# Seven half-size products from the seventh unit on in the second and third FFN of a two-layer hybrid model

## The chip, the cores and the metric

The kernel runs on one core of a Trainium2 chip. The metric is the device time of one execution in microseconds (us). The engines are PE (TensorE, matrix products; PEld is its weight load), DVE (VectorE), ACT (ScalarE), POOL (GpSimd) and SP (SyncE, which here only issues transfers). A transfer between the chip's memory (HBM) and the on-chip buffers is a DMA. Each engine works through its own queue in order; when an instruction waits, those behind it wait too.

## The reference

Two layers act on 256 latent tokens (LAT) and 256 context tokens (CTX), 1024 wide. Each layer is a half FFN, a mixer (attention in the first layer, an mLSTM in the second), and another half FFN; the mLSTM and the last FFN have an output for the latent tokens only. Nine modulation vectors per layer come from two condition vectors.

```python
def half_ffn(h, shift, scale, gate, w_in, w_out, g, b):
    xm = modulate(h, shift, scale)
    a, u = jnp.split(xm @ w_in, 2, axis=-1)
    y = (jax.nn.silu(a) * u) @ w_out
    return post_norm(h, 0.5 * gate * y, g, b)

for i in range(DEPTH):
    mod_lat = jnp.split((jax.nn.silu(c) @ ada_w[i] + ada_b[i])[:, None, :], N_MOD, axis=-1)
    mod_ctx = jnp.split((jax.nn.silu(c_ctx) @ ada_w[i] + ada_b[i])[None, None, :], N_MOD, axis=-1)
    h_lat = half_ffn(h_lat, mod_lat[0], mod_lat[1], mod_lat[2], ffn_w_in[i, 0], ffn_w_out[i, 0], ...)
    h_ctx = half_ffn(h_ctx, mod_ctx[0], ...)
    ...
    # mixer on modulated tokens, post_norm
    ...
    h_lat = half_ffn(h_lat, mod_lat[6], mod_lat[7], mod_lat[8], ffn_w_in[i, 1], ffn_w_out[i, 1], ...)
```

`w_in` is 1024 x 5632 (the halves `a` and `u`), `w_out` 2816 x 1024.

## The kernel before

**Precision.** A product of two float32 values is made of three passes in a reduced format (fp32r). Each operand is split into a high part (`h`, a rounding copy on ACT) and a low part (`l = x - h`, a subtraction on DVE): `split`, lines 221 to 227. `mm3` (line 236) then adds h h, h l and l h on PE. Weights arrive by a DMA on SP in chunks of 128 x 1024 values (512 KB) in `raw` buffers (`RAW`, three of them), and are split into a pair `w` (`WB`, seven of them).

**An FFN** (`ffn`, line 658) works on 22 units of 128 hidden columns, in two halves of 11 (`hf` 0 and 1). A full unit (`unit_in`) takes two weight chunks: 16 blocks of 128 x 128, each in three passes over all 512 tokens, 48 products of 512 columns. `ffn_g` makes silu(a) u and splits it. Behind each half, `unit_out` multiplies the 11 results by `w_out` for eight output blocks `d` of 33 products each. The first four units of the second and third FFN (LEAD) run on the latent tokens first and then on the context tokens, while the norm of the stage before still ends.

**Seven products.** In the second half (units 11 to 21) of the second and third FFN, `fast_in` (line 606) treats a unit as a 2 x 2 by 2 x 2 block product (a against u, lower against upper half of the 1024 inputs, latent against context tokens) with seven half-size products in place of eight. These are 7 x 4 x 3 = 84 products of 256 columns. It needs sums of weight blocks (line 615, four per unit, on DVE), all seven of them split (four splits), and sums of token blocks (`fast_sums`, line 579), which were made beside the output blocks 4 and 5 of the first half. At the end of a unit, lines 649 to 656 put the products together on DVE and ACT.

**Modulation.** Two layers of `ada_w` have 144 chunks of 512 KB. `ada` (line 343) loads one on SP into one of two `ada` buffers and forms a dot product on DVE for each condition vector (line 337). The 72 chunks of the second layer (112 dots) run inside the second and third FFN, as `DOTS` says: 4 or 3 dots per full unit, and some per output block. The silu of the condition vectors (`cb`) was held beside the `ada` buffers; that memory was given up for the token sums of `fast_in` and loaded again after each FFN.

**Order.** The kernel is written as one stream; a scheduler orders each engine's queue when it is built, by the order of the text and by when it expects operands and free buffers. `pin` keeps instructions in the order of the text. The residual (`residual`, line 536: DVE line 543, ACT line 544) runs as two per unit from unit 4 on. A weight pair is free once PE has made its last product with it; the next cast (line 222) waits for that.

**mLSTM** (`mlstm`, line 1146): queries, then keys (`jobs`, the convolution at lines 1179 and 1180), then values (line 1229), then a loop over eight head and direction units (`inner`, `outer`, `gated`; lines 1250 to 1324), then the output product.

Of the kernel before, what the change touches and what calls it, by code (L numbers as in the profile page):

```python
# [42 lines left out]
RAW = 3  # L43
# [92 lines left out]
def part_k(part, k):  # L136
    return k // 4 * 8 + part * 4 + k % 4


class Stream:  # L140


    def __init__(self, b, chunks, sh=0):
        self.b, self.chunks, self.kept = b, chunks, (None, None)
        self.sh = sh if callable(sh) else lambda c: sh

    def __call__(self, i, w=P):
        c, o = divmod(i * P, 1024)
        if self.kept[0] != c:
            self.kept = (c, self.b.chunk(self.chunks[c], self.sh(c)))  # L150
        h, l = self.kept[1]
        return h[:, o : o + w], l[:, o : o + w]
# [17 lines left out]
class Body:  # L170
# [44 lines left out]
    def chunk(self, src, sh=0):  # L215
        r = self.raw(src)
        h, l = self.pair(sh=sh)
        self.split(r, h, l)
        return h, l

# [48 lines left out]
    def setup(self):  # L269
# [13 lines left out]
        self.s1 = {}  # L283

    def silu_c(self):

        pool = ExitStack()
        self.n += 1
        p = pool.enter_context(self.tc.tile_pool(name=f"cp{self.n}", bufs=1, side="right"))
        self.cp = p  # L290
        self.cb = self.t([P, 2, D], pool=p)
        return pool
# [4 lines left out]

    def silu_all(self):
        pool = self.silu_c()
        self.silu_load()  # L300
        self.silu()
        return pool
# [24 lines left out]
    def ada_load(self, layer, dt):  # L327
        if (layer, dt // ND) not in self.mod:
            self.mod[layer, dt // ND] = self.t([P, 2, ND])
        r = self.t([P, 1024], tag="ada", bufs=2, pool=self.cp)  # L330
# [64 lines left out]
    def add_sum(self, g, d):  # L395
# [4 lines left out]
        if d == 0:  # L400
            self.s1[g] = self.t([P, TL], tag="s1", bufs=S1B)
# [21 lines left out]
    def norm(self, g, coef, keep=True, nxt=True, alone=False):  # L423
# [20 lines left out]
        for d in range(ND):  # L444
# [16 lines left out]
            else:  # L461
                a, s2 = sums[eng]
                s2 = s2 or self.t([P, TL], tag="s1", bufs=S1B)
# [30 lines left out]
        if most:  # L494
            dls = self.t([P, TL], tag="dl", bufs=1)
# [10 lines left out]
        if raw:  # L506
            S.copy(rs, rb[:, :w])
            dr = self.t([P, TL], tag="s1", bufs=S1B)
# [37 lines left out]

    def ffn_g(self, j, pa, pu, g, raw=False):
# [3 lines left out]
        if j not in self.gt:  # L551
            self.gt[j] = tuple(self.t([P, self.gw], F32R, tag=k, bufs=self.gn, pool=self.gp) for k in ("gh", "gl"))
        gh, gl = self.gt[j]
# [18 lines left out]
    def fast_operands(self, st):  # L572
# [3 lines left out]
        at = [2 * i * n + (FLIP if i == 2 else 0) for i in range(3)]  # L576
        self.made = [[x[:, a + p * n : a + (p + 1) * n].rearrange("p (k f) -> p k f", f=TL) for p in range(2)] for a in at]

    def fast_sums(self, i):
# [1145 lines left out]
```

## Time and profile before

| | |
|---|---|
| median of 3 runs | 1650.65 us (1648.48 to 1651.94) |
| the profiled execution | 1649.32 us, of it 1647.6 us from the first to the last instruction (the span) |
| granted PE clock, mean | 0.993 |
| products on PE | 10308 |
| read from HBM | 249.81 MB |
| first FFN, attention | to about 385, to about 590 us |
| second FFN, third FFN | to about 930, to about 1275 us |
| mLSTM, last FFN | to about 1460 us, to the end |

The profile is a record of one execution. In a list of groups, a row has the line, the engine, the operation, output and input, the shape and the count, then busy time, mean duration in ns and the idle time before it with what ended it. In a timeline, a row begins with the start and the length in us; an entry in brackets is the idle time of the engine before it and what it waited for. In windows, each engine's busy time in the stretch is followed by the number of its instructions. A duration is not always the distance to the next start: instructions of one engine overlap a little.

### The profile page before, as it was taken

The numbers are of one execution on the slowest core, as the hardware profiler recorded it, in microseconds if no ns is written. First come the engines' busy times: TensorE is split into PE (matmuls) and PEld (weight loads), VectorE is DVE, ScalarE is ACT, GpSimd is POOL, SyncE is SP. The second block draws the span as 40 slices with busy tenths as digits, with TensorE's granted clock in tenths as the row PEclk, the third lists the DMA queues.
The fourth block names the chain that finished last, engine by engine and source line by source line (L and its number), as shares of the span: only waits on it lengthen the run. The fifth ranks groups of instructions, "written<-read, shape, count | busy, mean of one in ns | idle before, by whom it ended". The sixth has DMA issues, their size and how long they took to land. (4 is left out here: it accounts for less than half of the span.)

```text
span 1647.6 us, 26587 instructions
## 1 busy us (share of the span) xinstructions
PE 1617.8 (98%) x10308; PEld 1457.4 (88%) x10308; DVE 1353.8 (82%) x2689; ACT 744.2 (45%) x1269; POOL 61.6 (4%) x76
## 2 busy tenths in 40 slices
PE   9999999999999999999999999899999999999998
PEld 6888888899988998889999998689999989999987
DVE  5899978649888879999977977799965968897687
ACT  5532222314676343425652433225652656656542
POOL 0000000001011200000000100000000100020000
PEclk9999999999999999999999999899999999999999
DMA  9577765622103247733353267733352342437652
GB/s 371 187 237 231 239 215 187 203 76 84 65 1 91 64 143 229 229 128 129 103 182 126 78 193 255 250 120 116 115 155 66 116 120 78 135 109 256 181 172 96
DMA packets 72495, 252.59 MB, mean 153 GB/s; under 512 B 7984, under 2 KB 10800, under 8 KB 72368
## 3 DMA queue, kind: packets, MB, share of 16 engines
q1 hardware_dynamic: 71792, 250.10, 47.8%
q8 instruction: 81, 1.33, 0.3%
q10 hardware_dynamic: 576, 0.79, 0.1%
q14 instruction: 46, 0.38, 0.1%
HBM read 249.81 MB, written 1.05 MB: 152 GB/s over the span
## 5 line engine op out<-in xcount | busy, mean ns | idle before, releaser
L238 PE MATMUL t<-t,t 128*128 128x256 f32 (+2 forms) x8412 | 1325.1, 319 | 14.2 <-ACT t L222 10.7
L238 PEld LDWEIGHTS t<-t,t 128*128 128x128 f32 x8412 | 1193.1, 189 | 133.9 <-ACT t L222 12.7
L222 ACT CAST t<-t 128x1024 fp32r<-128x1024 f32 (+3 forms) x521 | 429.6, 844 | 467.3 <-PE t L238 244.3
L227 DVE TENSOR_TENSOR t<-t,t 128x256 fp32r<-128x256 f32 (+2 forms) x740 | 514.7, 728 | 116.6 <-ACT t L222 112.5
L337 DVE SCALAR_TENSOR_TENSOR t<-t,t 128x1024 bf16<-128x1024 f32 x224 | 263.5, 1220 | 25.2 <-DMA t<-in_ada_w 24.5
L909 PE MATMUL t<-t,t 128*128 128x256 f32 (+1 forms) x256 | 79.5, 311 | 0.0
L911 PE MATMUL t<-t,t 128*128 128x256 f32 (+1 forms) x256 | 78.8, 308 | 0.0
L910 PE MATMUL t<-t,t 128*128 128x256 f32 (+1 forms) x256 | 78.4, 306 | 0.0
L568 ACT ACTIVATE t<-t 128x512 f32<-128x512 f32 (+1 forms) x71 | 34.3, 487 | 95.6 <-PE t L238 95.6
L692 DVE SCALAR_TENSOR_TENSOR t<-t,t,t 128x256 f32<-128x256 f32 x96 | 42.7, 478 | 37.0 <-PE t L238 37.0
L569 DVE TENSOR_TENSOR t<-t,t 128x512 f32<-128x512 f32 (+1 forms) x71 | 38.9, 551 | 32.8 <-PE t L238 26.7
L464 POOL TENSOR_TENSOR t<-t,t 128x256 f32<-128x256 f32 x30 | 23.4, 781 | 1130.9 <-ACT t L454 1129.7
L1424 PE MATMUL t<-t,t 128*128 128x512 f32 (+3 forms) x286 | 60.2, 365 | 2.0 <-ACT t L1501 1.0
L837 PE MATMUL t<-t,t 128*128 128x512 f32 (+1 forms) x300 | 60.7, 364 | 0.0
L1424 PEld LDWEIGHTS t<-t,t 128*128 128x128 f32 (+2 forms) x286 | 43.8, 159 | 18.3 <-issue 2.2
L837 PEld LDWEIGHTS t<-t,t 128*128 128x128 f32 x300 | 51.4, 189 | 9.1 <-DVE t L831 0.3
L454 ACT ACTIVATE t<-t 128x256 f32<-128x256 f32 x72 | 26.2, 411 | 72.3 <-DVE t L447 72.3
L544 ACT ACTIVATE t<-t,t 128x256 f32<-128x256 f32 x64 | 29.4, 503 | 57.4 <-DVE t L543 57.4
L909 PEld LDWEIGHTS t<-t,t 128*128 128x128 f32 x256 | 48.4, 189 | 2.7
L910 PEld LDWEIGHTS t<-t,t 128*128 128x128 f32 x256 | 48.2, 188 | 2.6
L911 PEld LDWEIGHTS t<-t,t 128*128 128x128 f32 x256 | 48.1, 188 | 2.5
L615 DVE TENSOR_TENSOR t<-t,t 128x512 f32<-128x512 f32 x66 | 45.3, 686 | 1.1 <-DMA t<-in_ffn_in 0.3
(200 smaller groups left out, 1065.5 us busy)
## 6 DMA issues: line engine op xcount, KB each, us to landing
t<-in_ffn_in SPq DMA_DIRECT2D x168, 512.0 KB, 4.1
t<-in_ada_w SPq DMA_DIRECT2D x137, 512.0 KB, 4.2
t<-in_ffn_out SPq DMA_DIRECT2D x66, 512.0 KB, 4.4
t<-in_ffn_last SPq DMA_DIRECT2D x22, 512.0 KB, 3.5
t<-in_att_in SPq DMA_DIRECT2D x12, 512.0 KB, 3.5
t<-in_c SPq DMA_DIRECT2D x8, 512.0 KB, 7.8
t<-in_att_out SPq DMA_DIRECT2D x8, 512.0 KB, 3.5
t<-in_ml_qk SPq DMA_DIRECT2D x8, 512.0 KB, 3.6
```

The costliest lines, as they stand in the source:

```text
L222: self.behind(self.nc.scalar.copy(h, x))
L227: self.behind(self.nc.vector.tensor_tensor(out=ls, in0=xs, in1=hs.bitcast(F32), op=ALU.subtract))
L238: mm = lambda *k, **kw: self.nc.tensor.matmul(*k, skip_group_check=not group, **kw)
L337: ins = nc.vector.scalar_tensor_tensor(self.tmp().bitcast(BF16), r, 1.0, self.cb[:, v, :], ALU.mult, ALU.mult, accum_out=to)
L569: V.tensor_tensor(out=sl, in0=sl, in1=pu[:, :n], op=ALU.mult)
L615: add = lambda o, x, y: V.tensor_tensor(out=o, in0=x, in1=y, op=ALU.add)
L692: V.scalar_tensor_tensor(z, y[:, gg[0] - t0 : gg[1] - t0], gate()[:, v, d : d + 1], z, ALU.mult, ALU.add)
L837: pin(nc.tensor.matmul(o, gs[g], ws[k][w][:, i : i + n], start=k == k0 and g == w == 0, stop=k == k1 - 1 and g == 1,))
L909: mm(o, self.xh[:, k, c], wh, start=k == 0, stop=False)
L910: mm(o, self.xh[:, k, c], wl, start=False, stop=False)
L911: mm(o, self.xl[:, k, c], wh, start=False, stop=k == ND - 1)
L1424: mm = lambda *k, **kw: pin(nc.tensor.matmul(*k, **kw))
```

## The change

1. `FIRST = 6`: in the second and third FFN, units 6 to 21 are made with seven products (before 11 to 21).
2. The token sums (`fast_sums`) are made in one piece behind the context tokens of the second unit, on 1024 values per operation, in memory of the later `g` tiles; the two whose place the full units still read are split at the end of unit 5 (`fast_last`). Unit 6 has its products in another order.
3. `ffn_in` lies by part: one chunk is all 1024 inputs of `a`, the next all of `u`. Full units run all of `a` before `u`; the opening units keep both chunks.
4. `fast_in` forms the weight sums in place. The low part of the first chunk isn't subtracted on DVE: `split_added` writes the negated copy by ACT, and a transfer issued by POOL adds the chunk to it, read again from HBM. Three chunks of `w_out` per half (`OUTADD`) go the same way.
5. `RAW` goes from 3 to 4. In the second FFN, third FFN and mLSTM, `ada` chunks use the `raw` buffers. `cb` stays in memory.
6. `DOTS`: one chunk at units 6, 8, 10, 12, 15, 18 and 21 and at most output blocks; 24 single dots go into the mLSTM (5 in the keys, 6 in the values, 13 in the head units).

```diff
-RAW = 3
+RAW = 4
...
-SUMSAT = 4
+FIRST = 6
+GONE = 7
 FLIP = 56
+OUTADD = (2, 5, 8)
 DOTS = {
-    1: {("in",): 4, ("out", 0): 3, ("out", 1): 2},
-    2: {("in",): 3, ("out", 0): 2, ("out", 1): 3},
+    1: {**{("in", j): 2 for j in (6, 8, 10, 12, 15, 18, 21)}, **{("out", 0, d): 2 for d in range(6)},
+        ("out", 0, 6): 4, ("out", 0, 7): 4, **{("out", 1, d): 2 for d in range(3)}, ("out", 1, 3): 4},
+    2: {**{("in", j): 2 for j in (6, 8, 10, 12, 15, 18, 21)}, **{("out", 0, d): 2 for d in range(6)},
+        ("out", 0, 6): 4, ("out", 0, 7): 4, **{("out", 1, d): 2 for d in range(3)}, ("out", 1, 3): 4},
+    "ml": {**{("key", n): 1 for n in range(5)}, **{("val", n): 1 for n in range(6)}, **{("unit", n): 1 for n in range(9)}, ("unit", 9): 2, ("unit", 10): 2},
...
-    return k // 4 * 8 + part * 4 + k % 4
+    return part * ND + k
...
+        if added:
+            self.split_added(r, h, l, src)
+        else:
+            self.split(r, h, l)
...
+    def split_added(self, x, h, l, src=None):
+        self.nc.scalar.copy(h, x)
+        self.nc.scalar.activation(l, x, AF.Copy, scale=-1.0)
+        self.nc.gpsimd.dma_start(l, x if src is None else src, accum_op=ALU.add)
...
+        if self.adas:
+            r = self.t([P, 1024], tag="ada", bufs=2, pool=self.adas)
+        else:
+            r = self.t([P, 1024], tag="raw", bufs=RAW)
...
+    def gtiles(self, j):
+        if j not in self.gt:
+            n, i = self.gw, j % NFH - GONE
+            if self.gn == NF or i < 0:
+                bufs = NF if self.gn == NF else GONE
+                self.gt[j] = tuple(self.t([P, n], F32R, tag=k, bufs=bufs, pool=self.gp) for k in ("gh", "gl"))
+            else:
+                assert i % 2 == 0
+                x = self.t([P, 4 * n], F32R, tag=f"g{i}", bufs=1, pool=self.gp)
+                for m in range(2):
+                    self.gt[j + m] = tuple(x[:, (2 * m + k) * n : (2 * m + k + 1) * n] for k in range(2))
+        return self.gt[j]
...
+    def fast_sums(self):
 
         V = self.nc.vector
-        lo, up = slice(2 * i, 2 * i + 2), slice(ND // 2 + 2 * i, ND // 2 + 2 * i + 2)
-        made = lambda k: [x[:, lo, :] for x in self.made[k]]
-        def at(ks, g):
-            return self.xh[:, ks, g[0] : g[1]], self.xl[:, ks, g[0] : g[1]]
-        def whole(ks, g):
-            o = self.tmp().rearrange("p (k f) -> p k f", k=2)
-            h, l = at(ks, g)
-            V.tensor_tensor(out=o, in0=h.bitcast(F32), in1=l.bitcast(F32), op=ALU.add)
-            return o
-        a, b = whole(lo, LAT), whole(lo, CTX)
-        V.tensor_tensor(out=a, in0=a, in1=b, op=ALU.subtract)
-        self.split(a, *at(lo, CTX))
-        c = whole(up, CTX)
-        V.tensor_tensor(out=b, in0=c, in1=b, op=ALU.subtract)
-        self.split(b, *made(1))
-        V.scalar_tensor_tensor(a, a, -1.0, c, ALU.mult, ALU.subtract)
-        self.split(a, *made(0))
-        d = whole(up, LAT)
-        V.scalar_tensor_tensor(d, a, -1.0, d, ALU.mult, ALU.subtract)
-        self.split(d, *made(2))
-    def fast_in(self, j, w_in, st):
+        lo, up = slice(0, ND // 2), slice(ND // 2, ND)
+        k = lambda x, i: x[:, i * 1024 : (i + 1) * 1024].rearrange("p (k f) -> p k f", f=TL)
+        x2, x1 = (self.t([P, 2048], tag=f"g{i}", bufs=1, pool=self.gp) for i in (0, 2))
+        t3, t2, t1, t4 = k(x2, 0), k(x2, 1), k(x1, 0), k(x1, 1)
+        add = lambda o, x, y, op=ALU.add: V.tensor_tensor(out=o, in0=x, in1=y, op=op)
+        less = lambda o, x, y: V.scalar_tensor_tensor(o, x, -1.0, y, ALU.mult, ALU.subtract)
+        def whole(o, ks, g):
+            add(o, self.xh[:, ks, g[0] : g[1]].bitcast(F32), self.xl[:, ks, g[0] : g[1]].bitcast(F32))
+        whole(t1, lo, LAT)
+        whole(t3, lo, CTX)
+        add(t1, t1, t3, ALU.subtract)
+        whole(t4, up, CTX)
+        add(t3, t4, t3, ALU.subtract)
+        less(t2, t1, t4)
+        whole(t4, up, LAT)
+        less(t4, t2, t4)
+        self.split(t3, *self.made[1])
+        self.split(t2, *self.made[0])
+        self.kept = t1, t4
...
+    def fast_last(self):
+        t1, t4 = self.kept
+        self.split(t1, *(x[:, : ND // 2, TL:T] for x in (self.xh, self.xl)))
+        self.split(t4, *self.made[2])
...
-        ws = [self.pair(sh=SH, n=half)] + [self.pair(sh=SH) for _ in range(3)]
-        self.split(a11, *ws[0])
-        self.split(r1, *ws[1])
-        add(s1, a21, a22)
-        add(s2, s1, a11)
-        self.split(sums[:, : 2 * half], *ws[2])
-        add(s4, s2, a12)
-        add(s3, a11, a21)
-        self.split(sums[:, 2 * half :], *ws[3])
...
+        (a11, a12), (a21, a22) = ([part(r, i) for i in range(2)] for r in (r0, r1))
+        w0, w1, w2, w3 = self.pair(sh=SH), self.pair(sh=SH), self.pair(sh=SH, n=half), self.pair(sh=SH)
+        add = lambda o, x: V.tensor_tensor(out=o, in0=o, in1=x, op=ALU.add)
+        self.split_added(r0, *w0, w_in[2 * j])
+        add(a11, a21)
+        add(a21, a22)
+        self.split(r1, *w1)
+        add(a22, a11)
+        add(a12, a22)
+        self.split(a22, *w2)
+        self.split(r0, *w3)
+        w = {n: [part(x, i) for x in p] for n, p, i in (
+            ("a11", w0, 0), ("a12", w0, 1), ("s1", w1, 0), ("a22", w1, 1), ("s2", w2, 0), ("s3", w3, 0), ("s4", w3, 1),
...
+        for f in (px, pz, pv) if first else (pv, px, pz):
+            f()
...
+                if g == BOTH:
+                    for part in range(2):
+                        for k in ks:
+                            self.mm3(o[part], w(part_k(part, k)), self.x(k, g), k == 0, k == ND - 1)
+                else:
+                    for k in ks:
+                        for part in parts:
+                            self.mm3(o[part][:, :n], w(part_k(part, k)), self.x(k, g), k == 0, k == ND - 1)
+                        self.steps(steps.get((j, k), ""))
+                if ks[-1] < ND - 1 or parts[-1] < 1:
                     return pa, pu
+                if late:
+                    late()
...
-                    ps = unit_in(j, ws[j], LAT, ks=k0)
+                    ps = unit_in(j, ws[j], LAT, parts=(0,))
                     assert not self.running
                     pc = unit_in(first[0], ws[first[0]], CTX, ks=k0)
                     ws[j](ND)
                     unit_in(first[0], ws[first[0]], CTX, ks=k1, ps=pc)
-                    unit_in(j, ws[j], LAT, ks=k1, ps=ps)
+                    unit_in(j, ws[j], LAT, parts=(1,), ps=ps)
...
+                        if fast and j == first[1]:
+                            self.npool.close()
+                            tpool, st = self.right()
+                            self.fast_operands(st)
+                            self.fast_sums()
...
+                    if fast and j >= FIRST:
+                        self.fast_in(j, w_in, j == FIRST)
+                    else:
+                        unit_in(j, stream(j), allg, late=self.fast_last if fast and j == FIRST - 1 else None)
...
+                w = Stream(self, [w_out[hf * NFH + i] for i in range(NFH)], added=OUTADD if fast else ())
...
+                self.some(DOTS["ml"].get(("key", n - MH), 0))
...
+                self.some(DOTS["ml"].get(("unit", n), 0))
```

More of the change, by code (lines that the diff above doesn't have):

```diff
@@ L638, in fast_in, with pv, px, pz @@
         a, u = self.tmp(), self.tmp()
+        def pv():
+            product(v, "s1", of(0, CTX), True, False)
+            S.copy(u[:, TL:], v)
+        def px():
+            product(x, "s2", made(0), False, False)
+            S.copy(a[:, TL:], x)
+        def pz():
+            product(z, "a22", made(2), True, True)
+            S.copy(u[:, :TL], z)
         product(x, "a11", of(0, LAT), True, False)
@@ L654, in fast_in, with ffn @@
         V.tensor_tensor(out=a, in0=a, in1=u, op=ALU.mult)
-        gh, gl = self.gt[j] = tuple(self.t([P, self.gw], F32R, tag=k, bufs=self.gn, pool=self.gp) for k in ("gh", "gl"))
-        self.split(a, gh, gl)
-    def ffn(self, layer, s, gate, groups, side, start=None, cpool=None):
+        self.split(a, *self.gtiles(j))
+    def ffn(self, layer, s, gate, groups, side, start=None, fast=False):
         nc, V = self.nc, self.nc.vector
@@ L1584, in emit @@
     b.setup_rest()
-    cpool = b.silu_c()
     both2 = (0, 1)
@@ L1607, in some @@
                 b.ada(*later.pop(0))
+            return later
+        b.some = some
         get = once(key, coef)
```

112 lines of the change are left out of this document (38 added, 74 removed).

## Prediction

> **What bounds the kernel now.** I read the head of the page first.
>
> ```profile
> span 1647.6 us, 26587 instructions
> ...
> PE 1617.8 (98%) x10308; PEld 1457.4 (88%) x10308; DVE 1353.8 (82%) x2689; ACT 744.2 (45%) x1269; POOL 61.6 (4%) x76
> ```
>
> TensorE (PE) is busy 98% of the span, so time comes off in two ways only: fewer columns through PE, or less of the 30 us in which it stands. The second view, the wait list of PE, says where it stands.
>
> ```profile
> PE t L238 <- ACT t L222: 10.7, 4, 7.5
> ```
>
> One wait of 7.5 us is most of what is named. The timeline around it (start, length, engine, operation) and two short windows (PE, PEld, DVE, ACT, POOL busy, then granted clock, DMA share, GB/s) show the whole stall. It lies in the third FFN, where the first half's last unit hands over to the w_out products.
>
> ```profile
> 1047.71 0.59 ACT L568 ACTIVATE t<-t 128x512 f32<-128x512 f32 x1
> ...
> 1049.25 1.22 DVE L337 SCALAR_TENSOR_TENSOR t<-t,t 128x1024 bf16<-128x1024 f32 x1
> 1050.40 0.08 DVE L337 DVE_READ_ACCUMULATOR t<-t,t 128x1 f32 x1
> ...
> 1053.98 1.23 DVE L337 SCALAR_TENSOR_TENSOR t<-t,t 128x1024 bf16<-128x1024 f32 x1 [2.37 <-DMA t<-in_ada_w]
> ...
> 1055.13 0.88 DVE L543 SCALAR_TENSOR_TENSOR t<-t,t,t 128x256 f32<-128x256 f32 x2
> ...
> 1055.93 0.68 DVE L569 TENSOR_TENSOR t<-t,t 128x512 f32<-128x512 f32 x1
> ...
> 1057.31 42.92 PE L238 MATMUL t<-t,t 128*128 128x512 f32 x177 [7.55 <-ACT t L222]
> ...
> 1055.00:1060.00 5.00, 2.69 (x6) 1.87 (x7) 4.32 (x9) 2.47 (x4) 0.00 (x0) 0.50 0.40 125
> 1060.00:1065.00 5.00, 5.00 (x19) 4.02 (x18) 4.22 (x9) 0.77 (x1) 0.00 (x0) 0.76 0.85 291
> ```
>
> The unit's SiLU is done at 1048.3, but its product on VectorE (L569) starts only at 1055.9, because modulation dots (L337) that wait for their own loads stand ahead of it on DVE. Then PE runs at a granted 0.50 until 1060 (2.7 us, half lost: 1.3) and at 0.76 until 1065 (5 us: 1.2 lost). The stall costs 7.55 + 2.5 = **10.1 us**. The page "TensorE: Matmul & The Clock Gate" of the Trainium skill (Part 1: The HAM clock gate) says that an idle array restarts at half rate for about 3.4 us; by it the loss behind the gap would be 1.7 us and the sum below 0.8 us later; the rows decide.
>
> The pace of PE comes from one operation per unit, followed over a stage: L568 in eleven full units, L649 in the eleven seven-product units of the second and of the third FFN.
>
> ```profile
> L568 ACT ACTIVATE t<-t x11: 598/598/600, 213.3 to 322.1; 128x512 f32<-128x512 f32 x11
> L649 DVE TENSOR_TENSOR t<-t,t x11: 676/679/683, 758.0 to 854.6; 128x512 f32<-128x512 f32 x11
> L649 DVE TENSOR_TENSOR t<-t,t x11: 677/680/681, 1122.7 to 1220.2; 128x512 f32<-128x512 f32 x11
> ```
>
> A full unit takes 108.8 / 10 = 10.88 us (48 products of 512 columns). A seven-product unit takes 96.6 / 10 = 9.66 and 97.5 / 10 = 9.75 us (84 products of 256). I use the slower, 9.75.
>
> **The change part by part.** Five more units (6 to 10) in each of two FFNs become seven-product units: 10 x (10.88 - 9.75) = **-11.3 us**, as long as PE still sets their pace. Whether it does is a matter of DVE, ACT and the adding transfer.
>
> DVE: its issue-to-issue times are shorter than its durations.
>
> ```profile
> 743.60 0.69 DVE L615 TENSOR_TENSOR t<-t 128x512 f32<-128x512 f32 x1
> 744.21 0.69 DVE L615 TENSOR_TENSOR t<-t,t 128x512 f32<-128x512 f32 x1
> ...
> 750.05 1.22 DVE L227 TENSOR_TENSOR t<-t,t 128x1024 fp32r<-128x1024 f32 x1
> 751.18 1.41 DVE L615 TENSOR_TENSOR t<-t,t 128x512 f32<-128x512 f32 x2
> ...
> 1120.00:1215.00 95.00, 95.00 (x821) 95.00 (x821) 86.18 (x113) 59.30 (x98) 0.00 (x0) 1.00 0.38 113
> ```
>
> 512 elements take 0.60, 1024 take 1.13, and a residual pair (L543 x2, above) 0.80 us. A unit before has nine 512s and three 1024s: 8.8 us (the window has 86.18 / 95 x 9.75 = 8.8). After, one 1024 goes to the adding transfer and a 512 split goes with it, while the s2 operand is split as a 512: four sums, two 1024 lows, two 512 lows and three operations at the end, 7.7 us. Units 6 to 10 also carry a residual pair each (4.0 in all) and three chunks of two dots (L337 to its read-out above: 1.15 us, so 2.4 with the read-out): 38.3 + 4.0 + 7.2 = 49.5 us against 48.8 of PE. DVE is 0.8 us short per FFN, 1.6 in both: I take **+2**. The ends are 0, since the w_out products behind leave DVE room, and 14.4, if all dots stand in the way. Units 11 to 21 need 11 x 7.7 + 4 x 2.4 = 94 of 107 us: nothing.
>
> ```profile
> L222 ACT CAST t<-t 128x1024 fp32r<-128x1024 f32 x309 | 323.3, 1050 | 355.3 <-PE t L238 227.3 <-issue 70.4 <-DMA t<-in_ffn_in 20.3
> ...
> 1167.40 0.37 ACT L645 COPY t<-t 128x256 f32<-128x256 f32 x1 [0.99 <-PE t L238]
> 1167.67 0.63 ACT L222 CAST t<-t 128x512 fp32r<-128x512 f32 x1
> ...
> DMA to landing us min/median/max: 3.4/4.2/10.0
> ```
>
> ACT gains one 1.05 us pass per unit (the negated copy): 59.30 / 95 x 9.75 = 6.1 becomes 7.1 of 9.75 us, hidden under PE. The **adding transfer** has no row before: POOL issues no transfer. Its deadline is readable. The first cast of a unit (the 512 at 1167.67) comes right after the copy of a fourth product, when PE frees a weight slot. Seven slots, of which two stay with the running unit and four with the next, put that cast two units ahead: 3/7 + 1 units, 13.9 us, before its product. Less two ACT passes of 1.05, the transfer has 11.8 us. Plain 512 KB loads (the last row, of in_ada_w) land in 3.4 to 10.0 us; one that must also read its target could take twice that, so 3.4 to 20. I take 7, nearer to the median doubled than to its worst, and so **0 us**; if the cover is gone, each us beyond 11.8 costs 7/10 us per unit, in 30 units. The page "DMA: Bandwidth & Descriptors" of the Trainium skill (Anatomy of one DMA) fits 2.0 us plus bytes over 436 GB/s for a transfer of GpSimd, an estimate of 3.2 us, for plain copies; by it too the term is 0. The w_out lows given to the same path have longer cover (a chunk lasts 8 x 3 products), and what else stands in POOL's queue, the norms' operations, fills 4% of the span.
>
> The **token sums** move from the w_out stage to the opening: eight 1024s and two lows, 11.3 us, where 16 dots go (16 x 1.15 = 18.4). Where these dots ran, DVE was full and PE was not held:
>
> ```profile
> 610.00:655.00 45.00, 45.00 (x206) 37.46 (x205) 42.71 (x71) 14.06 (x21) 0.00 (x0) 1.00 0.75 230
> ```
>
> So 0. The last two splits wait for PE at the end of unit 5 and stand behind 5.6 us of products that don't need them (four of seven, 9.75 x 4/7): 0; uncovered, 4.4 per FFN (two ACT and two DVE passes). Weight chunks that now hold one part need two chunks before the first product of a stage: one low of 1.13 us in three openings, 0 to 3.4; **+1**. Dropping the second load of c and its SiLU takes work from engines that nobody waits for: 0.
>
> The **stall** of 10.1 us: its two causes, two to three chunks at each unit and two buffers for them, both change (one chunk at unit 10, four buffers shared with the weights). I take **-10.1**; the ends are 0 and -10.1.
>
> The **24 dots** left over go into the mLSTM, 24 x 1.23 = 29.5 us of DVE.
>
> ```profile
> 1310.00:1360.00 50.00, 50.00 (x250) 42.03 (x250) 34.02 (x51) 29.16 (x40) 0.00 (x0) 1.00 0.43 127
> 1360.00:1430.00 70.00, 69.32 (x511) 65.91 (x510) 57.98 (x174) 47.34 (x104) 3.65 (x8) 1.00 0.30 95
> ...
> 1430.41 0.88 DVE L1324 SCALAR_TENSOR_TENSOR t<-t,t,t 128x256 f32<-128x256 f32 x2 [1.74 <-PE t L1321]
> ```
>
> Eleven (13.5 us) fall among keys and values, where DVE has 16 us free: 0. Thirteen (16.0 us) fall into the head units, where it has 12.0 us free: 4.0 over, and one more dot ahead of the last gating (L1324), which ends the stage. **+5**; ends 0 and 29.5. Their loads stand in SP's queue between the mLSTM's weights, where the DMA share (0.43, 0.30) leaves room.
>
> **Sum**, on the profiled execution's 1649.3 us (its span 1647.6 and 1.7 around it): 1649.3 - 11.3 - 10.1 + 2 + 1 + 5 = 1635.9. It lay 1.3 below the median of the runs, so I predict **1637**.
>
> **Rivals.** *Dots hidden*: the dots and the short DVE in units 6 to 10 cost nothing: 1637 - 7 = 1630. For it speaks that PE is full from 1310 to 1360 and lacks 0.7 us in the next 70, so DVE may lag; against it, only 12 us are free there. *The stall stays* or comes in another FFN: 1637 + 10 = 1647, with one each in both FFNs 1657. For it: DVE is short in units 6 to 10. Against it: the second FFN had four dots per unit and no such wait. *The adding transfer is late*: from 11.8 us on PE waits at each first product; at 13 us 30 x 0.7 x 1.2 = 25 us, 1662, slower than before. For it: its target must be read and no row prices it; against it: DMA share 0.38 there. *Dots on the chain*: if all the 24 hold PE, 1637 + 24.5 = 1661, slower than before; from 18.4 us unhidden (11.3 + 10.1 - 3) the change loses; against it: 16 us are free among the values.
>
> **How the numbers follow.** A difference within 0.2% (3.3 us, 1647.3 to 1654) can't be told from no change. Chances: forecast 0.50, dots hidden 0.12, stall stays 0.14 (half faster, a third the same, the rest slower), late transfer 0.14, dots on the chain 0.10 (a fifth of it the same). So faster 0.69, same 0.07, slower 0.24. The likeliest case alone spans 1629 to 1645. The range reaches down to 1626 (7 us of costs and some clock loss besides gone) and up to the late transfer's 1662.
>
> **What would show it.** Units 6 to 10 at 9.75 us by the distance of their last VectorE products; PE's wait for the cast at the turn to w_out gone, with no clock below 0.9 between 600 and 1300 us; adding transfers done within 11.8 us and no PE wait for them at a first product; the head units of the mLSTM some 5 us longer. I am wrong if PE waits for the adding transfer in each unit, if a new wait of over 5 us stands in the mLSTM, or if units 6 to 10 take over 10.2 us.

## The result, and the profile after

The changed kernel takes **1782.7 us** (median of four runs, 1779.8 to 1786.8) against 1650.6 for the kernel before: a ratio of 1.0804, 95% interval 1.0779 to 1.0828. It is slower by 132 us, where 1637 was forecast and 1662 was the slow end. The profiled execution has a span of 1781.5 us, 133.9 over before. The page of the kernel after, its head and three lines of its DMA issues (the last number is the median time from issue to landing):

```profile
span 1781.5 us, 27498 instructions
...
PE 1655.0 (93%) x10668; PEld 1503.0 (84%) x10668; DVE 1360.1 (76%) x2703; ACT 803.3 (45%) x1356; POOL 99.2 (6%) x118
...
t<-in_ada_w SPq DMA_DIRECT2D x137, 512.0 KB, 4.1
...
t<-in_ffn_in POOLq DMA_DIRECT2D x32, 512.0 KB, 6.6
...
t<-in_ffn_out POOLq DMA_DIRECT2D x10, 512.0 KB, 8.1
```

PE now stands 126 us instead of 30, and its busy time grew by 37 us although there are fewer columns to multiply: the granted clock fell from a mean of 0.993 to 0.962. VectorE was busy hardly longer than before (1360.1 against 1353.8 us), so it is not more work there that costs the time. PE's list of waits (total, times, longest) says what it waits for:

```profile
PE t L251 <- DMA t<-in_ffn_in: 61.1, 17, 6.1
PE t L251 <- ACT t L235: 29.9, 11, 10.2
PE t L251 <- DMA t<-in_ffn_out: 6.7, 1, 6.7
```

A weight that PE gets straight from a DMA can only be a low part made by an adding transfer, since all others pass through ScalarE and VectorE. The pace shows where: one VectorE operation of each seven-product unit (L684 here, L649 before), for units 6 to 10 and units 11 to 21 of the second and then of the third FFN.

```profile
L684 DVE TENSOR_TENSOR t<-t,t x5: 680/681/689, 644.1 to 682.3; 128x512 f32<-128x512 f32 x5
L684 DVE TENSOR_TENSOR t<-t,t x11: 679/689/689, 760.9 to 900.3; 128x512 f32<-128x512 f32 x11
L684 DVE TENSOR_TENSOR t<-t,t x5: 679/683/689, 1050.9 to 1089.1; 128x512 f32<-128x512 f32 x5
L684 DVE TENSOR_TENSOR t<-t,t x11: 682/687/689, 1167.5 to 1306.5; 128x512 f32<-128x512 f32 x11
```

Units 6 to 10 take 38.2 / 4 = 9.55 us each; 9.75 was forecast. The units of the second halves take 139.4 / 10 = 13.9 us, where they took 9.7 before. The length of each stage, from the first and last sums of the w_out products on VectorE (L692 before and L735 after; L898 and L937 for the mLSTM), accounts for the whole difference:

| stage, us | before | after | difference |
|---|---|---|---|
| to the second FFN's first w_out sum | 696.8 | 691.6 | -5.2 |
| its first w_out | 52.9 | 52.2 | -0.7 |
| its units 11 to 21 | 116.0 | 166.1 | +50.1 |
| its last w_out | 55.0 | 61.5 | +6.5 |
| third FFN, units 0 to 10 | 139.5 | 127.1 | -12.4 |
| its first w_out | 54.5 | 52.1 | -2.4 |
| its units 11 to 21 | 116.3 | 164.8 | +48.5 |
| its last w_out | 55.2 | 75.2 | +20.0 |
| mLSTM | 167.1 | 196.2 | +29.1 |
| the rest | 194.3 | 194.7 | +0.4 |

The second FFN's second half as one window, after and then before (PE, PEld, DVE, ACT, POOL busy, then granted clock, DMA share, GB/s):

```profile
743.00:910.00 167.00, 136.12 (x965) 132.03 (x964) 107.64 (x156) 81.72 (x126) 10.51 (x12) 0.87 0.54 136
```

```profile
749.00:866.00 117.00, 116.85 (x960) 114.69 (x960) 102.18 (x138) 70.53 (x116) 0.00 (x0) 1.00 0.44 139
```

The same matmuls took 116.9 us of PE before. Now PE stands 167 - 136.1 = 30.9 us and needs 136.1 - 116.9 = 19.2 us more for them at a clock of 0.87. So the 50 us are three parts standing still and two parts the slow clock behind it. The timeline of two such units shows the loop (start, length; in brackets the idle time before and what ended it):

```profile
823.23 1.05 ACT L230 CAST t<-t 128x1024 fp32r<-128x1024 f32 x1
824.18 1.05 ACT L231 ACTIVATE t<-t 128x1024 fp32r<-128x1024 f32 x1
...
825.64 0.87 POOL L232 DMA_DIRECT2D t<-in_ffn_in  x1 [9.28 <-ACT t L679]
...
834.93 12.17 PE L251 MATMUL t<-t,t 128*128 128x256 f32 x82 [3.70 <-DMA t<-in_ffn_in]
837.47 0.37 ACT L679 COPY t<-t 128x256 f32<-128x256 f32 x1 [6.20 <-PE t L251]
837.74 2.08 ACT L235 CAST t<-t 128x512 fp32r<-128x512 f32 x3
...
841.30 0.37 ACT L668 COPY t<-t 128x256 f32<-128x256 f32 x1 [1.48 <-PE t L251]
841.57 1.05 ACT L230 CAST t<-t 128x1024 fp32r<-128x1024 f32 x1
842.52 1.06 ACT L231 ACTIVATE t<-t 128x1024 fp32r<-128x1024 f32 x1
...
843.99 0.87 POOL L232 DMA_DIRECT2D t<-in_ffn_in  x1 [17.48 <-ACT t L672]
...
849.54 1.79 PE L251 MATMUL t<-t,t 128*128 128x256 f32 x10 [2.45 <-DMA t<-in_ffn_in]
```

The transfer issued at 825.64 lands at 834.93, and PE had been ready since 834.93 - 3.70 = 831.23: it had a lead of 5.6 us and took 9.3. Since PE was late, ScalarE's copy of the first product (L679) came 6.2 us late, and behind it in ScalarE's order stood the casts, a second copy that waits for PE, and only then the copy and negated copy of the next unit (841.57, 842.52). So the next transfer went out at 843.99, with PE ready at 847.09: a lead of 3.1 us instead of 5.6. One late transfer makes the next one late: PE waits for one in 17 of the 22 units of the two second halves. What makes the first one late is a load:

```profile
742.60 1.05 ACT L230 CAST t<-t 128x1024 fp32r<-128x1024 f32 x1 [11.10 <-DMA t<-in_ffn_in]
745.01 0.87 POOL L232 DMA_DIRECT2D t<-in_ffn_in  x1 [27.65 <-ACT t L231]
```

ScalarE stands 11.1 us for unit 11's chunk (12.1 in the third FFN), and its transfer goes out only at 745.01. Unit 6, in the same order, had its transfer issued at 612.31, 23 us ahead of ScalarE's copy of its first product (635.28), and unit 10 still 11 us ahead (664.86 and 675.75); PE waited for no transfer of units 6 to 10.

The other two losses, in the timeline of SP's queue and of PE (third FFN's last w_out, then the mLSTM):

```profile
1327.87 6.77 SPq L344 DMA_DIRECT2D t<-in_ada_w  x4
1349.11 6.63 SPq L212 DMA_DIRECT2D t<-in_ffn_out  x5
...
1342.49 5.04 PE L251 MATMUL t<-t,t 128*128 128x512 f32 x20 [6.74 <-DMA t<-in_ffn_out]
1353.94 13.64 PE L251 MATMUL t<-t,t 128*128 128x256 f32 x97 [6.41 <-ACT t L235]
...
1393.32 10.45 SPq L344 DMA_DIRECT2D t<-in_ada_w  x3
...
1435.20 1.22 PE L251 MATMUL t<-t,t 128*128 128x512 f32 x2 [10.21 <-ACT t L235]
...
1519.70 21.24 SPq L344 DMA_DIRECT2D t<-in_ada_w  x5
...
1550.71 9.57 SPq L212 DMA_DIRECT2D t<-in_ml_out  x7
```

Four loads for dots go out from 1327.87 on, through the four raw buffers, and w_out's next chunks are asked for only 21 us later. In the mLSTM five such loads take from 1519.70 to 1540.94, and the first chunk of its output weights is asked for at 1550.71. In the windows of the two mLSTM stalls PE is busy for less than half and the clock is low:

```profile
1420.00:1440.00 20.00, 9.51 (x32) 6.89 (x32) 18.79 (x32) 9.95 (x13) 0.00 (x0) 0.68 0.39 125
1540.00:1560.00 20.00, 8.14 (x50) 7.05 (x49) 18.57 (x49) 8.56 (x15) 0.70 (x1) 0.67 0.66 231
```

### The profile page after: what moved, and what is told of

It is laid out like the page before. It is cut to its first block, busy times and chain, and to the rows that moved or that the text cites. A ratio compares the mean times of both kernels' runs of the same rounds, so it can differ in the third digit from the quotient of the medians.

```text
span 1781.5 us, 27498 instructions
## 1 busy us (share of the span) xinstructions
PE 1655.0 (93%) x10668; PEld 1503.0 (84%) x10668; DVE 1360.1 (76%) x2703; ACT 803.3 (45%) x1356; POOL 99.2 (6%) x118
## 5 line engine op out<-in xcount | busy, mean ns | idle before, releaser
L251 PE MATMUL t<-t,t 128*128 128x256 f32 (+2 forms) x8772 | 1361.4, 317 | 106.0 <-DMA t<-in_ffn_in 61.1
L251 PEld LDWEIGHTS t<-t,t 128*128 128x128 f32 x8772 | 1239.5, 195 | 216.0 <-DMA t<-in_ffn_in 64.5
L235 ACT CAST t<-t 128x1024 fp32r<-128x1024 f32 (+3 forms) x491 | 398.3, 836 | 496.7 <-issue 127.8
L240 DVE TENSOR_TENSOR t<-t,t 128x256 fp32r<-128x256 f32 (+2 forms) x710 | 481.1, 713 | 159.7 <-ACT t L235 156.7
L350 DVE SCALAR_TENSOR_TENSOR t<-t,t 128x1024 bf16<-128x1024 f32 x224 | 263.5, 1220 | 5.4 <-DMA t<-in_ada_w 5.1
L643 DVE TENSOR_TENSOR t<-t,t 128x512 f32<-128x512 f32 x96 | 66.0, 687 | 28.4 <-ACT t L231 27.1
L735 DVE SCALAR_TENSOR_TENSOR t<-t,t,t 128x256 f32<-128x256 f32 x96 | 42.7, 479 | 57.3 <-PE t L251 57.2
L230 ACT CAST t<-t 128x1024 fp32r<-128x1024 f32 x42 | 44.0, 1049 | 56.7 <-DMA t<-in_ffn_out 25.1
L593 DVE TENSOR_TENSOR t<-t,t 128x256 f32<-128x256 f32 (+1 forms) x61 | 32.2, 532 | 48.8 <-PE t L251 29.9
L876 PEld LDWEIGHTS t<-t,t 128*128 128x128 f32 x300 | 51.5, 189 | 8.9
L232 POOL DMA_DIRECT2D t<-in_ffn_in x32 | 28.2, 883 | 487.0 <-ACT t L672 101.7
L592 ACT ACTIVATE t<-t 128x256 f32<-128x256 f32 (+1 forms) x61 | 28.1, 470 | 52.6 <-PE t L251 51.3
L948 PEld LDWEIGHTS t<-t,t 128*128 128x128 f32 x256 | 48.4, 189 | 2.7
L949 PEld LDWEIGHTS t<-t,t 128*128 128x128 f32 x256 | 48.1, 188 | 2.5
L950 PEld LDWEIGHTS t<-t,t 128*128 128x128 f32 x256 | 48.1, 188 | 2.5
```

The costliest lines, as they stand in the source:

```text
L230: self.nc.scalar.copy(h, x)
L235: self.behind(self.nc.scalar.copy(h, x))
L240: self.behind(self.nc.vector.tensor_tensor(out=ls, in0=xs, in1=hs.bitcast(F32), op=ALU.subtract))
L251: mm = lambda *k, **kw: self.nc.tensor.matmul(*k, skip_group_check=not group, **kw)
L350: ins = nc.vector.scalar_tensor_tensor(self.tmp().bitcast(BF16), r, 1.0, self.cb[:, v, :], ALU.mult, ALU.mult, accum_out=to)
L643: add = lambda o, x: V.tensor_tensor(out=o, in0=o, in1=x, op=ALU.add)
```

## The experiments

Every experiment starts from the changed kernel. Runs without an interval are single executions; the kernel before, on the same chips, took 1650.2 to 1653.0 us.

**Units without the adding transfer.**

```
-        self.split_added(r0, *w0, w_in[2 * j])
+        self.split(r0, *w0)
```

> The low part of each unit's first weight chunk is made on VectorE again; the adding transfers of the w_out chunks stay. Theory A (each unit's negated copy is issued only once the unit before it has started, so that the adding transfer of 6 us lands after PE is ready for it): the eleven units of the second half go from 13.9 us back to between 9.6 and 10.0 us in both FFNs, no wait of PE for a transfer at a first product, and the time falls by 22 x 4.1 = 90 us, to 1685 to 1700. Rival B (the weights' loads come late, since four raw buffers are shared with the dots' loads): PE waits for the casts of those loads instead, the second half stays at 13 us or more and the time at 1765 or above. Rival C (VectorE can't take the low of 1.13 us back, four of eleven units carry dots): 11.0 us per unit or more, 1710 to 1730.

1731.9 us, 51 less: well below rival B's 1765, 32 us above theory A's range and 2 above rival C's. The second halves fell from 166.1 and 164.8 us to 135.2 and 134.9; the two last w_out stages grew by 6.5 and 1.7. The units' pace, and the timeline around one unit with a pair of dots (L350):

```profile
L684 DVE TENSOR_TENSOR t<-t,t x11: 680/681/691, 761.5 to 871.1; 128x512 f32<-128x512 f32 x11
```

```profile
807.99 1.22 DVE L350 SCALAR_TENSOR_TENSOR t<-t,t 128x1024 bf16<-128x1024 f32 x1
...
810.28 1.41 DVE L643 TENSOR_TENSOR t<-t,t 128x512 f32<-128x512 f32 x2
...
811.67 0.50 PE L251 MATMUL t<-t,t 128*128 128x256 f32 x2 [1.45 <-ACT t L235]
812.40 28.93 PE L251 MATMUL t<-t,t 128*128 128x256 f32 x229 [0.22 <-DVE t L240]
```

That is 10.96 us per unit: steps of about 10 us, one of 11.6, and two of 14.3 where the dots stand on VectorE ahead of the weight sums (L643) that PE needs next. In such a step PE stands some 2 us, and the clock falls behind it (0.64 from 812 to 816 us). So the adding transfers cost some 60 us in the second halves, but 38 us (2 x 19) of the loss there have another cause.

**w_out without it.**

```
-OUTADD = (2, 5, 8)
+OUTADD = ()
```

> The adding transfers of the three w_out chunks in each half are replaced by a low on VectorE, those of the units stay. Theory A (the same lateness in the third FFN's second w_out half only, where one wait of 6.7 us for an adding transfer stands): PE's wait there goes, the clock loss behind it too: 5 to 12 us less, 1771 to 1778. Rival B (there the w_out loads themselves are late, behind four loads for dots in SP's queue, as the next wait of 6.4 us for a cast says): the wait only changes its name, 1780 to 1785.

1774.2 us, 8.5 less, within theory A. Four executions of the changed kernel differ by up to 7 us, so the stage says it better: the third FFN's last w_out falls from 75.2 to 67.3 us. It had 55.2 before, so 12 us of it were not the transfer.

**The mLSTM's dots in the opening units.**

```
-    1: {**{("in", j): 2 for j in (6, 8, 10, 12, 15, 18, 21)},
+    1: {**{("in", j): 2 for j in (0, 1, 2, 3, 4, 5, 6, 8, 10, 12, 15, 18, 21)},
...
-    "ml": {**{("key", n): 1 for n in range(5)}, **{("val", n): 1 for n in range(6)}, **{("unit", n): 1 for n in range(9)}, ("unit", 9): 2, ("unit", 10): 2},
+    "ml": {},
```

> The 24 modulation dots leave the mLSTM for the first six full units of the second and of the third FFN, two to each. Theory A (in the mLSTM the dots' loads stand in SP's queue ahead of its weights, two waits of 10 us at a lower clock, and the dots delay the last splits): the mLSTM gets back some 29 us, units 0 to 5 lose at most 5, and the time falls to 1755 to 1762. Rival B (the mLSTM is longer for another reason, such as the shared raw buffers or the pools that were moved): 1778 to 1785 and PE's two waits stay. Rival C (the loads in the opening collide with the units' weights there): the mLSTM gains and the openings lose as much, 1770 to 1785.

1864.8 us, 82 **more**: outside all three. The mLSTM did get back its 30 us (166.0, before 167.1), as theory A says. But the stretch up to the second FFN's first w_out sum grew by 30.5 us, the third FFN's units 0 to 10 by 24.7, its first w_out by 20.5 and its second half by 22.5. In the last two no dot was moved: by the code, the last 32 entries of `later` make one dot from a 512 KB load where the first 40 make two, and taking dots earlier brought those into the third FFN's first w_out and second half. A dot costs VectorE 1.2 us wherever it stands, but in the shared ring its load also takes a weight's buffer; that this is what costs is argued here, and tested further down.

**All three edits at once.**

> No adding transfer at all, and the 24 dots in units 0 to 5: the three edits above at once. If the three losses are separate, the sum holds: 1782 less 90 (units) less 8 (w_out) less 27 (mLSTM) = 1657, between 1640 and 1665; units 6 to 10 at 9.6 us leave 11 us of gain, so that below 1650 is possible. If VectorE becomes the bound in the second half once it makes all the lows (8.8 us per unit and 2.4 for each pair of dots, against 9.75), the pace there is 10.2 us or more and the time 1665 to 1685.

1758.1 us: both ranges missed. Without any adding transfer the third FFN's second half still takes 149.3 us and the openings 720.7 and 149.5. What the dots do, to the weights' loads or on VectorE, is thus a loss of its own.

**A buffer of their own for the dots' loads, no adding transfer.**

```
-        return self.t([P, 512], tag="tmp", bufs=6)[:, :w]
+        return self.t([P, 512], tag="tmp", bufs=5)[:, :w]
...
-            r = self.t([P, 1024], tag="raw", bufs=RAW)
+            r = self.t([P, 1024], tag="ada", bufs=1)
```

> No adding transfer, and the dots' loads get one buffer of their own instead of sharing the four raw ones (one of six temporaries is given up for its room); the dots stay where the change put them. By the two runs before, the kernel without adding transfers would take 1782 - 51 - 8 = 1723. Theory B (dots and weights hold up each other's loads in the shared ring, in the w_out stages, the openings and the mLSTM): the w_out stages and the mLSTM recover, 1660 to 1690, the mLSTM's span from the last w_out sum to its own last sum at most 185 us instead of 196. Rival C (VectorE is short wherever a pair of dots stands, whatever the buffers): 1715 to 1730, with the same steps of 14.3 us at the units with dots. Rival D (SP's queue is what holds the weights: a dot's load waits there for its one buffer, with the weights' loads behind it): slower than 1735.

1675.6 us, 47 below the 1723 that the kernel without adding transfers would have by the first two runs: theory B, but for the third FFN's last w_out. The second halves are 118.1 and 119.5 us, the step of 14.3 us is gone (rival C), and the unit's pace, one new wait of PE with what stands before it on VectorE, and a row of SP's waits read:

```profile
L684 DVE TENSOR_TENSOR t<-t,t x11: 675/680/689, 759.3 to 855.6; 128x512 f32<-128x512 f32 x11
```

```profile
1256.69 1.23 DVE L350 SCALAR_TENSOR_TENSOR t<-t,t 128x1024 bf16<-128x1024 f32 x1 [2.86 <-DMA t<-in_ada_w]
...
1258.83 1.22 PE L440 MATMUL t<-t,t 128*128 128x256 f32 x2 [5.07 <-DVE t L417]
```

```profile
SPq L344 <- DMA t<-in_ada_w: 109.9, 53, 4.1
```

The pace is 9.63 us. What is left lies where dots with one load each stand close together: 69.0 us in the third FFN's last w_out (67.3 with the shared buffers), 182.5 in the mLSTM, 201.7 behind it. With one buffer SP waits for a load to land before it can ask for the next (110 us in all), and the weights behind it wait too; at 1258.83 the next norm's first matmul waits 5 us for a sum (L417) that stands on VectorE behind a dot whose load came 2.9 us late.

**The buffer taken from the raw ones.** Three raw buffers, one for dots, six temporaries.

> As the last, but the buffer for dots is the fourth raw one (three are left for weights, six temporaries). If a unit that sums in place holds its two raw buffers so long that three are not enough, the second halves go from 10.9 to above 12 us per unit and the time lies 20 us or more over the last run's; if not, within 8 us of it.

1681.8 us, 6 more, hardly beyond the spread of single executions: the second halves take 121.0 and 120.0. So the fourth raw buffer is worth at most 3 us in one half and nothing in the other. With four buffers in all, as in the run with plain units (135.2 and 134.9), it was sharing them that cost.

**The adding transfer, earlier.** The changed kernel with all its transfers; in each unit the next one's loads, weight slot, copy, negated copy and transfer (the new function) come before the s2 cast, which the new argument holds behind them. Units 6 and 11, which open a stretch, are not ahead.

```
         self.split(r1, *w1)
+        if (j + 1) % NFH:
+            self.ahead[j + 1] = self.fast_ahead(j + 1, w_in)
         add(a22, a11)
...
-        self.split(a22, *w2)
+        w2, w3 = self.pair(sh=SH, n=half), self.pair(sh=SH)
+        self.split(a22, *w2, (j + 1) % NFH)
```

> The changed kernel with its adding transfers; only the place of each unit's copy, negated copy and transfer is moved: they stand on ScalarE ahead of the s2 cast of the unit before, so that the transfer is issued about a whole unit (9.7 us) before its product instead of 3 to 6 us. Theory A (the transfer costs only by its lateness): the second halves go from 13.9 to 9.7 to 11 us per unit, 1715 to 1740, and PE's waits for adding transfers in the units fall from 61 us to below 15. Rival B (the raw buffer that the copy reads is itself late, since two units hold all four): the waits move to the copies, the pace stays above 12.5, and the time at 1760 or more.

1738.5 us, as theory A has it. The pace, PE's wait for the units' transfers, and in the timeline the issue of two transfers:

```profile
L693 DVE TENSOR_TENSOR t<-t,t x11: 678/680/689, 769.1 to 877.8; 128x512 f32<-128x512 f32 x11
```

```profile
PE t L252 <- DMA t<-in_ffn_in: 13.7, 4, 6.0
```

```profile
803.73 0.88 POOL L232 DMA_DIRECT2D t<-in_ffn_in  x1 [8.82 <-PE t L252]
814.25 0.87 POOL L232 DMA_DIRECT2D t<-in_ffn_in  x1 [9.64 <-ACT t L231]
```

The same 32 transfers with the same ScalarE passes now stand in units of 10.87 us; they go out a unit apart, PE's waits for them fell from 61.1 to 13.7 us in four waits, and the second halves are 135.7 and 136.0 us, as long as with no adding transfer at all (135.2 and 134.9). So it was the lateness, not the transfer, that cost 60 us there. Of the 13.7 us, 11.8 stand at the two units 11, which are not ahead, and the units behind them catch up. The openings lost 12.7 us (698.8 and 132.6), which is why the whole gained only 44.

**Early transfers and the dots' own buffer together** (none in w_out).

> The last but one and the last together: adding transfers in the units a unit ahead, none in w_out, dots in one buffer of their own, five temporaries. If both theories hold, it lies below the kernel with plain lows and its own buffer, since VectorE is spared 1.1 us per unit: 10 to 25 us below that run. If the dots or SP's queue still decide, within 8 us of it.

1678.9 us, the same as with plain lows (1675.6) within the spread of single executions: the pass that VectorE is spared buys nothing. PE now waits 15.3 us in 13 short waits for ScalarE's copy of the first product, where it was 3.0 us in four. The transfers in their old place with a buffer of their own for the dots were not run, so how much of the 60 us the shared buffers set off, through the late chunk of unit 11, stays open.

**Two buffers for the dots, three raw ones, no adding transfer, five temporaries.**

> No adding transfer, three raw buffers for weights, two buffers of their own for the dots' loads, five temporaries: the dots stay where the change put them. In the run with one own buffer the third FFN's last w_out stage (69.0 us, before 54.8), the mLSTM (182.5, before 167.5) and what follows it (201.7, before 194.3) were still long, and there SP's queue waited 110 us for that one buffer's loads to land, one after the other. Theory B (late loads, nothing else): with two in flight these three come back to within 3 us of before each, second halves cost some 3 us each over before, and the total is 1676 - 36 + up to 6 = 1640 to 1650. Rival C (VectorE's 24 dots in the mLSTM and the ten in w_out are too much work there): the mLSTM stays above 175 us, the total above 1660.

Ratio 1.0035 (1.0019 to 1.0051): some 6 us over before, above theory B's range. The last w_out of the third FFN is cured (56.6 us), the mLSTM takes 171.8 and what follows 200.1, so theory B holds for the first and in good part for the second; the 5.8 us behind come back two runs below.

**The same, with the mLSTM's dots in the opening units.**

> The last, with the 24 dots of the mLSTM in the first six full units of the second and third FFN. With the shared ring this move cost 113 us in the two FFNs and gave 30 in the mLSTM. Theory B (only the sharing made it dear): the mLSTM at 166 to 168 us, the openings at most 5 us longer, total 1632 to 1645. Rival C (VectorE has the token sums there, 11 us in each FFN, and no room for 14 us of dots beside them): the openings 10 us longer or more, total 1650 to 1670.

Ratio 1.0082 (1.0067 to 1.0097). The mLSTM is at 167.0 and the rest at 194.2, but the opening of the second FFN takes 706.0 us (694.7 in the run above) and that of the third 134.2 (128.3): 17 us lost for 11 gained. With buffers of their own the dots are still dear beside the token sums; VectorE is busy 96.1 of the 106 us from 600 to 706: rival C in the second FFN, half of it in the third, and the total in its range.

**Fourteen of them in the w_out blocks instead,** where VectorE has room; the second FFN's last w_out takes two more in its first block.

```
-    1: {**{("in", j): 2 for j in (6, 8, 10, 12, 15, 18, 21)}, **{("out", 0, d): 2 for d in range(6)},
-        ("out", 0, 6): 4, ("out", 0, 7): 4, **{("out", 1, d): 2 for d in range(3)}, ("out", 1, 3): 4},
...
+    1: {**{("in", j): 2 for j in (6, 8, 10, 12, 15, 18, 21)}, **{("out", 0, d): 2 for d in (3, 4, 5)},
+        **{("out", 0, d): 4 for d in (0, 1, 2, 6, 7)}, ("out", 1, 0): 4, ("out", 1, 1): 2, ("out", 1, 2): 2, ("out", 1, 3): 4},
...
+    "ml": {**{("key", n): 1 for n in range(5)}, **{("val", n): 1 for n in range(5)}},
```

> The run with two own buffers (no adding transfer, three raw buffers, five temporaries), with 14 of the mLSTM's 24 dots, those of its head units and one of its values, moved to the second and third FFN's first w_out blocks and one block of the second's last w_out. There the mLSTM was 4.7 us over before and what follows it 5.8. Theory (those are the dots of the head units, which VectorE does late, and the norm behind waits): the stretch after the mLSTM falls from 200 to 194 to 196 us, the mLSTM from 172 to 167 to 170, the w_out stages lose at most 3: total 1644 to 1650, faster than before by 0 to 0.4%. Rival (the added loads of 512 KB in the w_out stages hold up w_out's own): w_out stages 5 us longer or more, total 1654 to 1662.

1650.7 us median; ratio 0.9985 (0.9973 to 0.9997) over five rounds: the stretch behind the mLSTM is back at 194.7 us, the mLSTM at 171.0, and the w_out stages lost 3 in all, as the theory has it but for 1 us in the mLSTM and 0.7 in the total. It is the best version, 0.15% under before, less than the 0.2% that I call a difference.

**And those of the second FFN's second half.**

> The last, with the eight dots of the second FFN's second-half units moved to its w_out blocks too; the third FFN keeps its own, for comparison in one run. Theory (VectorE is short at units with dots once it makes all the lows): the second FFN's second half falls from 121 us to 116 to 118, the third's stays at 121, total 2 to 4 us under the last run. Rival (the pace there is held by the longer chain of sums in place, not by the dots): both stay at 121, and the total is the same or, with 32 dots in one w_out stage, 3 to 6 us more.

Ratio 1.0015 (1.0003 to 1.0027): the rival. Without any dot the second FFN's second half takes 124.8 us, the third's, with its dots, 121.8. The pace of both, then two waits in the second FFN's:

```profile
L684 DVE TENSOR_TENSOR t<-t,t x11: 677/681/682, 755.8 to 861.1; 128x512 f32<-128x512 f32 x11
L684 DVE TENSOR_TENSOR t<-t,t x11: 679/680/689, 1119.9 to 1220.1; 128x512 f32<-128x512 f32 x11
```

```profile
DVE t L643 <- DMA t<-in_ffn_in: 6.5, 9, 0.9
...
PE t L251 <- DVE t L240: 3.9, 10, 0.7
```

10.53 us per unit with no dot, 10.02 with four pairs: the dots are not what holds the pace. In the second FFN the sums in place wait 0.7 us per unit for a load, and PE waits 0.4 for the low behind them. A unit holds two raw buffers from its first sum to its last cast, so with three of them the next unit's second load may be late. With four raw buffers and one for dots the pace was 9.63, which speaks for this, but it is not shown: the third FFN had the same three buffers, and why the units without dots are the slower ones no run says. Four raw buffers and two for dots together were not tried.

## Why the prediction was wrong, step by step

**Right: the gains.** The ten more seven-product units were put at -11.3 us, the stall and its slow clock at -10.1, VectorE's shortness and the two-chunk openings at +3: -18.4. Measured, in the four stages up to the first w_out's end of both FFNs, -20.7 (5.2 + 0.7 + 12.4 + 2.4 us less). Units 6 to 10 run at 9.55 us, and the wait at the turn to w_out is gone.

**Wrong: the adding transfer at 0 us.** The step that failed is "Seven slots, of which two stay with the running unit and four with the next, put that cast two units ahead ... the transfer has 11.8 us". A free slot does not issue a copy. The copy waits for its chunk and stands in ScalarE's order behind copies that wait for PE, and the leads were 5.6 and 3.1 us in the two units shown. The transfer's own time was taken as 7 and measured 6.6. The rival of the late transfer named the right wait for another reason, a transfer of more than 11.8 us, and priced it at 0.84 us per unit (0.7 x 1.2) where the units of the second halves lost 4.2 (13.9 - 9.7), of which some 2.7 (60 / 22) went with the transfer's lateness. It lacked that the transfer goes out late, that the lateness feeds itself and that the clock halves behind the gaps. What shows it: moved ahead, 28 of the 32 transfers give back the 60 us, as leaving them out does. The w_out lows, put at 0 for their longer cover, cost another 8 us (75.2 against 67.3).

The page "DMA: Bandwidth & Descriptors" of the Trainium skill (Anatomy of one DMA), by whose fit 3.2 us was given for the 512 KB, does not agree with the 6.6 us measured; its fit has no term for a transfer that adds.

**Wrong: the four shared buffers as a relief.** The prediction counted "one chunk at unit 10, four buffers shared with the weights" among the reasons why the stall goes, and never as a cost. With the transfers out of the way 2 x 19 us were still lost in the second halves, 12 in the third FFN's last w_out and 29 in the mLSTM; two buffers of their own for the dots gave back 14 of each 19, 11 of the 12 and 24 of the 29.

**Wrong: the mLSTM at +5.** Its mechanism (VectorE 4.0 us short among the head units) missed the larger one. "Their loads stand in SP's queue between the mLSTM's weights, where the DMA share (0.43, 0.30) leaves room" took room on the wires for room in the queue. Measured +29.1; without the dots 0 (166.0 against 167.1); with two buffers of their own +4.7, which is about the forecast, but by luck: with no dot left in the head units it was still +3.9 (171.0 against 167.1), with only ten among the keys and values, which the forecast put at 0. The dots of the head units showed behind the mLSTM instead, +5.8 there with them and +0.4 without, which was not foreseen.

**The signs named beforehand.** Two of the three ways to be wrong came true: PE waits for the adding transfer in 17 of the 22 units of the second halves, and new waits of over 5 us stand in the mLSTM. The clock was below 0.9 in both second halves (0.87 and 0.88), where the forecast had it full.

## What to carry to other kernels

A deadline is set by where the instruction stands in its engine's order, not by when its buffer comes free: look for what it is queued behind, and whether that waits for the very engine which needs it. Loads of side work that share a ring with weights cost more than their bytes, since an unfinished side task holds a weight's buffer and its load blocks the queue; count loads per useful operation too. A step forecast at nothing because it is hidden deserves a bound for the case that it is not, with the feedback in it.

## What the runs showed of the hardware

A gap's length alone does not say what it costs in clock. Three windows of the changed kernel, then three of the run with the early transfers:

```profile
819.67:823.08 3.41, 2.11 (x18) 2.11 (x19) 3.41 (x7) 2.02 (x3) 0.00 (x0) 1.00 0.16 31
829.91:833.32 3.41, 1.32 (x12) 1.11 (x10) 3.40 (x5) 0.63 (x1) 0.00 (x0) 1.00 1.01 274
833.32:840.15 6.83, 5.22 (x24) 5.22 (x25) 2.42 (x5) 2.35 (x4) 0.00 (x0) 0.50 0.03 11
```

```profile
792.00:795.41 3.41, 2.16 (x16) 1.75 (x15) 3.41 (x6) 3.25 (x6) 0.87 (x1) 1.00 0.01 2
826.13:829.54 3.41, 1.74 (x13) 1.34 (x12) 3.41 (x7) 3.16 (x6) 0.87 (x1) 1.00 0.45 53
829.54:832.95 3.41, 3.41 (x19) 3.41 (x18) 2.48 (x4) 1.44 (x3) 0.00 (x0) 0.50 1.05 278
```

After a gap of 1.49 us, ended at 820.97, the clock stayed at 1.00; after one of 3.70, ended at 834.93, it was 0.50 for 5 us. In the other run three gaps of 0.25, 1.00 and 0.65 us, the last ended at 796.39, left it at 1.00, and three of 0.58, 1.02 and 0.65, the last ended at 829.04, halved it. The page "TensorE: Matmul & The Clock Gate" of the Trainium skill (Part 1: The HAM clock gate) has the gate watch a free-running window of about 3.4 us. The runs agree: the two half-rate stretches shown last 3.41 and 6.83 us, one and two such windows. Counted in steps of 3.41 us back from where the clock halves, PE was busy 1.32 and 1.74 us of the window just before; where the clock stayed full, it had been busy 2.11 and 2.16 us of a window. In these four it is PE's busy share of a window that parts them: the gaps of 1.02 and 0.65 us that halved the clock lay in one window, those of 1.00 and 0.65 that did not lay in two. They are too few for a threshold.

The adding transfer of 512 KB landed in 6.6 us (median) in the units of the changed kernel and in 5.4 in the run that issues it earlier, against 4.1 for a plain load from SP; those for w_out took 8.1, and POOL was busy 0.87 us with issuing one.
